# The S5 input projection channel-major, with its recurrence rows gathered through DRAM

## The chip, the cores and the metric

The kernel runs on one core of one Trainium2 chip. The metric is the time of one execution on the device in microseconds (us), as the median of several runs. A lower time is better. The engines are named as in the profile: PE is the matrix engine, PEld its weight loads, DVE the vector engine, ACT the scalar engine, POOL GpSimd. SP is SyncE, which issues every DMA of this kernel in one queue.

## The reference

The trunk has two layers on 512 tokens of 1024 channels, in float32. Each layer has three mixers beside each other and an MLP:

```python
for l in range(DEPTH):                                   # 2 layers
    z = _rmsnorm(x, norm_mix_g[l]) @ w_in[l]             # 1024 -> 2508 columns
    q, k, v, qi, ki, wi, u5, z_ssd, xbc, dt_raw = _split(z, IN_SIZES)
    attn_out = _dsa_mixer(q, k, v, qi, ki, wi, ...)      # 8 heads; an indexer keeps the top 128 keys
    s5_out = _s5_mixer(u5, ...)                          # 256 channels = 16 groups of 16
    ssd_out = _ssd_mixer(z_ssd, xbc, dt_raw, ...)
    x = x + concat(attn_out, s5_out, ssd_out) @ w_out[l]
    x = x + relu(_rmsnorm(x) @ w_up[l]) ** 2 @ w_down[l]
```

The S5 mixer runs, in every group of 16 channels, a diagonal complex recurrence of 64 states over the 512 tokens, reads it out, adds `d_skip * u`, and passes the result through gelu and a gated linear unit (GLU).

## The kernel before

**Order of the work.** The kernel is written as generators, one for each strand (the projection slab by slab, the S5 strand, the SSD strand, attention, the top-k of the indexer). A planner at build time advances whichever strand its own costs, priorities and due times choose, and so fixes the order of the instructions on every engine. On the chip each engine then works through its list in that order, and an instruction whose input is late holds up all behind it. The plan of the slices is `kv, xa, qi, q, xb, u5, z` in layer 0 and `kv, xa, qi, z, u5, q, xb` in layer 1.

**Products.** Weights come in slabs of 256 KB (`wraw`, line 159). ACT writes the high part (`whi`, line 171), DVE the low part (`wlo`, line 172); three raw and five split slabs are held. Each product of 128 rows is three matmuls (`mm3`, lines 436 to 438). `gemm_tok` gives token-major tiles, with 128 tokens as the stationary operand and the columns of the slab moving. `gemm_chan` gives channel-major tiles of 128 channels by 512 tokens, with 128 columns of the slab stationary and 512 tokens moving. Four PSUM banks (`pm`) hold the tiles of the projection.

**The S5 input before.** The slice `u5` (256 columns) is token-major, in four tiles whose tokens lie four apart. They leave PSUM at line 1186 (`usb`, on ACT), scaled per token by `rsp`, for which the strand sums squares once more (`tsum`, line 397) and takes a reciprocal root on DVE (`rsqrt`, lines 299 to 305).

**The S5 strand** (`s5`, line 671) works on chunks of 8 tokens. It wants `U`, two tiles for 8 groups each, whose row is (token within the chunk, channel within the group) and whose columns are groups by 64 chunks. Before, PE transposes `usb` (line 684) and ACT copies the halves out (lines 687 and 688). Then come the chunk sums on PE (`s5v`, line 699), ACT's evictions (`sv`, `svs`), a rotation and eight scans for each half on DVE (lines 714 to 726, which end in the two `X` tiles), PE's read-out (`s5y`, lines 738 and 739), the transposes back, gelu and the GLU (lines 750 to 775).

**Around it.** The table matrices `M` are zeroed by POOL (line 663) and filled by eight DMAs each from `strip` (line 666). The last `M` of layer 1 takes over a slot that `s5v` reads. The indexer's scores are `isc`; a round of its top-k is one MAX and one MATCH_REPLACE on DVE (lines 1076 and 1077), 16 rounds for each of the blocks 1, 2 and 3 of 128 tokens, and line 1080 makes the mask that attention waits for.

Of the kernel before, what the change touches and what calls it, by code (L numbers as in the profile page):

```python
# [10 lines left out]
F32 = mybir.dt.float32  # L11
# [11 lines left out]
NB = S // P          # token blocks  # L23
KC = D // P          # channel chunks of the trunk
# [83 lines left out]
# constants  # L108
# [8 lines left out]
# W_in slices: (first column, width), in the host's column order  # L117
# [17 lines left out]
class Slabs:  # L135
    """slabs of weight matrices in the order of their use: loaded and split into hi and lo parts some way ahead"""
# [44 lines left out]
    def take(self, n, tiles, outer):  # L181
        """the next n slabs for each of some tiles, as (tile, slab number, hi, lo): slab by slab if outer, else
        tile by tile, and then those to follow are split while the last tile uses these up"""
        if outer:
            for j in range(n):
                hi, lo = self.next()[0]
                for t in range(tiles):
                    yield t, j, hi, lo
            return
        cur = []  # L190
        for t in range(tiles):
            for j in range(n):
                if t == 0:
                    cur += self.next()
                elif t == tiles - 1:
                    self.load(self.i + AHEAD[0] + j)
                    self.split(self.i + AHEAD[1] + j)
                yield t, j, cur[j][0], cur[j][1]


class Net:
    def __init__(self, ctx, tc, a, taps=None):
# [91 lines left out]
    def rsqrt(self, y, x, n, eng=None):  # L294
        """y = 1/sqrt(x), [P, n] small"""
# [11 lines left out]
    def stt(self, v, out, x, s, y, op0, op1):  # L307
        """out = (x op0 s) op1 y, [P, n] small; GpSimd takes two instructions for it"""
# [7 lines left out]
    def expacc(self, out, x, t, v):  # L316
        """out = exp(x) to about an ulp, [P, n] small"""
# [15 lines left out]
    def sincos(self, c, s, th, t, v):  # L333
        """c, s = cos(th), sin(th), [P, n] small"""
# [14 lines left out]
        self.stt(v, q, q, 1.0, r, ALU.add, ALU.mult)      # sin(th/2)  # L349
# [4 lines left out]
        # cos(th/2) = 1 + w  # L354
# [9 lines left out]
    def norm_chunk(self, c, squares=True):  # L364
        """hi and lo parts of x*g, and the sum of squares over channels (still per partition)"""
# [25 lines left out]
    def token_sums(self, acc, perm=False):  # L391
        """[P, 4]: mean square + eps per token; block b is tokens b*128 + m, or with perm 4m + 3-b"""
        nc = self.nc
        p = self.ps("a", (P, 4), name="tsum")
        v = acc.rearrange("p (m f) -> p f m", f=4)
        for b in range(NB):
            nc.tensor.matmul(p[:, b:b + 1], v[:, 3 - b, :] if perm else acc[:, b * P:(b + 1) * P], self.ones[:, 0:1],
                             start=True, stop=True)
# [4 lines left out]
    def bcast_tokens(self, colv, k):  # L403
        """[P, 4] per-token columns -> psum tile [P, 512] with the token's value on every partition"""
# [6 lines left out]
    def add_slabs(self, l):  # L411
        """the weights of a layer, in the order of their use"""
# [20 lines left out]
    def mm3(self, p, lh, ll, rh, rl, first, last):  # L433
        """p += (lh+ll)^T (rh+rl), without the product of the two low parts (below float32's last bit)"""
# [5 lines left out]
    def gemm_tok(self, ps, xh, xl, slabs, sls):  # L440
        """token-major blocks: psum tile of block i [tok, n] = ps(i), tokens sls[i]; yields (cost, finished tile)"""
# [14 lines left out]
    def gemm_chan(self, ps, slabs, xh, xl):  # L456
        """channel-major tiles of 128 columns of a slice of 256: [chan, tok]; yields (cost, finished tile)"""
# [13 lines left out]
    def s5_small(self):  # L471
        """powers of the discretised state matrix and the input matrices, both layers"""
# [38 lines left out]
        # powers 0..8  # L511
# [17 lines left out]
        # X = (pr; pi), Y = (-pi; pr) on the two halves of the partitions  # L529
# [8 lines left out]
        # m8 and the rotation of one chunk, with the angle's sign turned on the lower half  # L538
# [4 lines left out]
        self.rot = []          # e^{+-i phi 2^k}  # L543
# [22 lines left out]
    def s5_tables(self, l, t):  # L566
        """the matrices of one layer's chunked recurrence, into t"""
# [29 lines left out]
        def outer(v, out, u, w, u2, w2, gs, d0, d1):  # L597
            """out[g, d, h] = u[g, h] w[g, d] + u2[g, h] w2[g, d]"""
# [9 lines left out]
        for q in range(4):  # L608
# [4 lines left out]
            BPp = self.tt([P, 4, 8, 16], name="BPp")               # d = 1..8: the states stand one step ahead  # L613
            outer(v, BPp, bbr, X, bbi, Y, gs, 1, 9)
            # transposed input powers: rows (d, h')
# [8 lines left out]
        # rotations by chunk  # L624
# [21 lines left out]
        for q in range(4):  # L646
            v = eng(f"C{q}")
            gs = slice(4 * q, 4 * q + 4)
            ca = self.tt([P, 4, 8, 16], name="CA")                 # d = 0..7
# [7 lines left out]
            # the skip term joins the kernel's first tap  # L657
# [14 lines left out]
    def s5(self, l, tab, usb, out):  # L672
        """usb: token-major input -> hi/lo of the two channel-major output tiles"""
# [5 lines left out]
        # input with rows (d = 7-i, h')  # L679
        U = [self.h([P, 8, C5], name="U5") for _ in range(2)]  # L680
        for q4 in range(4):
            p = self.ps(self.bank["sU"], (64, 4, P), name="s5U")
            for j in range(4):
                nc.tensor.transpose(p[:, j], usb[q4 // 2][:, (4 * q4 + j) % 8].rearrange("p b h -> p (b h)"), self.ident)
            pv = p.rearrange("p g (c e) -> p g c e", e=2)
            o = slice(4 * (q4 % 2), 4 * (q4 % 2) + 4)
            nc.scalar.activation(U[q4 // 2][0:64, o], pv[:, :, :, 1], AF.Copy)
            nc.scalar.activation(U[q4 // 2][64:128, o], pv[:, :, :, 0], AF.Copy)
            yield self.pace["s5"] * 1.0
# [38 lines left out]
        # rows (half of the groups, chunk)  # L728
# [16 lines left out]
        # channel-major, columns (token of the chunk, half, chunk)  # L745
        gg = []
        for jh in range(2):
# [8 lines left out]
            v.scalar_tensor_tensor(t, t, 1.0, p, ALU.add, ALU.mult)      # 2 gelu(y)  # L756
# [25 lines left out]
    def ssd(self, l, r_, out):  # L782
# [3 lines left out]
        # step sizes  # L786
# [37 lines left out]
        # convolution and silu, each with half the argument  # L824
        xc = {}
        for m in (0, 1, 2, 3) if self.plan["w_order"].index("xa") < self.plan["w_order"].index("xb") else (2, 3, 0, 1):
# [16 lines left out]
            else:  # L843
                # C of each group, with zeros on the other group's partitions
# [21 lines left out]
            # token-major inputs  # L866
# [12 lines left out]
            # scores  # L879
# [33 lines left out]
        # gate and group norm  # L913
# [55 lines left out]
    def head_ms(self, out, src, nh):  # L969
        """mean square over the 64 of each head, + eps"""  # L970
# [6 lines left out]
    def rope(self, x, rs, c, s):  # L977
        """x = rope(x * rs * gain), of the keys"""
# [8 lines left out]
    def rope_q(self, x, c, s):  # L987
        """the rotated part of eight heads' queries"""
# [8 lines left out]
    def attn_keys(self, l, ksb, rt):  # L997
        """ksb: [P, 3, 64] per block (k0 k1 ki): norm, rope, transposes"""
# [7 lines left out]
        # hi and lo parts of the keys, each on both halves of the partitions  # L1006
# [18 lines left out]
    def transpose_heads(self, src):  # L1025
        """[P, 8, 64] token-major -> per head [P (hi d, lo d), P tokens]"""
# [15 lines left out]
    def head_dot(self, p, q, K, i, nk):  # L1042
        """p[tok, key] = q . k, both with all of their bits"""
# [3 lines left out]
    def index_scores(self, b, qi, K, wi, accs):  # L1047
        """masked scores of block b (>= 1): [P, (b+1)*128]"""
# [21 lines left out]
    def topk_masks(self, accs):  # L1070
        """the 128 largest of each row (lowest index first among equals) keep 0, the rest get NEG"""
# [10 lines left out]
    def attend(self, b, qT, K, mask, nrs, ah, al):  # L1082
        """nrs: minus the scale of each head's logits"""
# [450 lines left out]
```

## Time and profile before

| | us |
|---|---|
| median of 3 runs (1359.14 to 1361.53) | 1359.96 |
| span of the profiled execution | 1356.7 |
| difference, taken as fixed time around the span | 3.3 |
| layer 0: mixers, MLP | 0 to 355, 355 to 715 |
| layer 1: mixers, MLP | 715 to 985, 985 to 1357 |
| PE busy over the span | 1247.9 (92%) |
| DVE busy over the span | 883.2 (65%) |
| mean granted clock of PE, as a share of full speed | 0.967 |

The profile shows one execution. Busy times are sums over the span, and a share that is high over the whole can be low in one stage. The record of one matmul is longer than the distance between the starts of two, since matmuls overlap; so a row of matmuls is priced by the starts.

### The profile page before, as it was taken

How to read it: one execution, taken by the hardware profiler on the slowest of the kernel's cores; microseconds unless marked ns; L12 is line 12 of the kernel's file. 1: busy time of each engine (PE TensorE's matmuls, PEld its weight loads, DVE VectorE, ACT ScalarE, POOL GpSimd, SP SyncE). 2: the span in 40 equal slices, each digit the busy share in tenths (PEclk: the TensorE clock that was granted, in tenths of full speed). 3: DMA queues.
4: the chain of work that ended last, by engine and by line, in shares of the span. 5: the costliest groups of instructions: out<-in, count | busy, mean ns of one | idle time of the engine just before them, and what ended most of it. 6: DMA issues, size and time to landing. Idle time of an engine off the chain costs nothing. (4 is left out here: it accounts for less than half of the span.)

```text
span 1356.7 us, 17071 instructions
## 1 busy us (share of the span) xinstructions
PE 1247.9 (92%) x5852; PEld 1013.6 (75%) x5852; DVE 883.2 (65%) x2044; ACT 564.6 (42%) x1160; POOL 161.6 (12%) x301
## 2 busy tenths in 40 slices
PE   6679966879999999999999998978999999999998
PEld 5667854647888877888888897755688888888887
DVE  6899799884844544444466779998575444445443
ACT  4346352563542332423444535656454233242331
POOL 2593268200000221000000000000000000000000
PEclk9789987899999999999999998989999999999999
DMA  6122120001233323323323312100123333333332
GB/s 193 47 78 71 25 68 11 32 1 47 86 95 100 94 83 94 101 96 99 94 84 89 100 31 53 63 16 16 35 83 102 95 99 94 101 94 101 93 108 86
DMA packets 102694, 103.74 MB, mean 76 GB/s; under 512 B 10960, under 2 KB 95696, under 8 KB 102608
## 3 DMA queue, kind: packets, MB, share of 16 engines
q1 hardware_dynamic: 102608, 102.66, 25.1%
q8 instruction: 46, 0.75, 0.2%
q14 instruction: 40, 0.33, 0.1%
HBM read 99.36 MB, written 2.10 MB: 75 GB/s over the span
## 5 line engine op out<-in xcount | busy, mean ns | idle before, releaser
L172 DVE TENSOR_TENSOR wlo<-wraw,whi 128x512 fp32r<-128x512 f32 (+1 forms) x368 | 253.8, 691 | 300.6 <-ACT whi L171 298.4
L171 ACT ACTIVATE whi<-wraw 128x512 fp32r<-128x512 f32 (+1 forms) x368 | 229.0, 624 | 498.5 <-PE pm L437 332.4
L436 PE MATMUL pm<-xh,whi 128*128 128x512 f32 x608 | 239.8, 395 | 2.7 <-ACT usb L1186 1.1
L437 PE MATMUL pm<-xl,whi 128*128 128x512 f32 x608 | 238.5, 393 | 0.0
L438 PE MATMUL pm<-xh,wlo 128*128 128x512 f32 x608 | 238.4, 393 | 0.0
L438 PE MATMUL pm<-uh,wlo 128*128 128x512 f32 x512 | 199.5, 390 | 1.2 <-DVE wlo L172 1.2
L437 PE MATMUL pm<-ul,whi 128*128 128x512 f32 x512 | 199.7, 390 | 0.0
L436 PE MATMUL pm<-uh,whi 128*128 128x512 f32 x512 | 199.6, 390 | 0.0
L436 PEld LDWEIGHTS pm<-xh,whi 128*128 128x128 f32 x608 | 115.2, 190 | 27.6 <-ACT q L1210 1.6
L438 PEld LDWEIGHTS pm<-xh,wlo 128*128 128x128 f32 x608 | 115.1, 189 | 24.4 <-issue 0.3
L437 PEld LDWEIGHTS pm<-xl,whi 128*128 128x128 f32 x608 | 115.3, 190 | 23.1 <-DVE xl L372 0.2
L438 PEld LDWEIGHTS pm<-uh,wlo 128*128 128x128 f32 x512 | 96.2, 188 | 21.7 <-DVE wlo L172 1.6
L436 PE MATMUL pm<-whi,xh 128*128 128x512 f32 (+2 forms) x240 | 94.1, 395 | 19.8 <-ACT xh L370 12.4
L437 PEld LDWEIGHTS pm<-ul,whi 128*128 128x128 f32 x512 | 96.2, 188 | 20.3 <-issue 0.4
L436 PEld LDWEIGHTS pm<-uh,whi 128*128 128x128 f32 x512 | 96.2, 188 | 19.9 <-issue 0.2
L437 PE MATMUL pm<-wlo,xh 128*128 128x512 f32 (+2 forms) x240 | 92.5, 386 | 2.3 <-DVE wlo L172 2.3
L438 PE MATMUL pm<-whi,xl 128*128 128x512 f32 (+2 forms) x240 | 92.2, 388 | 1.5 <-DVE xl L372 1.4
L436 PEld LDWEIGHTS pm<-whi,xh 128*128 128x128 f32 x240 | 55.9, 234 | 27.1 <-ACT xh L370 12.8
L437 PEld LDWEIGHTS pm<-wlo,xh 128*128 128x128 f32 x240 | 56.3, 235 | 7.6 <-DVE wlo L172 3.4
L438 PEld LDWEIGHTS pm<-whi,xl 128*128 128x128 f32 x240 | 55.7, 234 | 7.1 <-DVE xl L372 2.5
L1384 DVE SCALAR_TENSOR_TENSOR ur<-pm,ur 128x512 f32<-128x512 f32 x64 | 44.0, 687 | 25.5 <-ACT ur L1381 25.5
L1392 DVE TENSOR_TENSOR sq<-pm,r2b 128x512 f32<-128x512 f32 x64 | 44.2, 690 | 23.2 <-PE pm L438 23.2
(349 smaller groups left out, 1915.2 us busy)
## 6 DMA issues: line engine op xcount, KB each, us to landing
wraw<-in_w_up_dram SPq DMA_DIRECT2D x128, 256.0 KB, 2.7
wraw<-in_w_down_dram SPq DMA_DIRECT2D x128, 256.0 KB, 2.7
wraw<-in_w_in_dram SPq DMA_DIRECT2D x64, 256.0 KB, 2.7
wraw<-in_w_out_dram SPq DMA_DIRECT2D x32, 256.0 KB, 2.7
wraw<-in_w_in_dram SPq DMA_DIRECT2D x16, 166.0 KB, 2.3
x<-in_xT_dram SPq DMA_DIRECT2D x8, 256.0 KB, 5.9
out_dram<-x SPq DMA_DIRECT2D x8, 256.0 KB, 2.0
s5bc<-in_s5bc_dram SPq DMA_DIRECT2D x4, 256.0 KB, 4.7
```

What stands on the lines that cost most here:

```text
L171: nc.scalar.activation(hi, raw, AF.Copy)
L172: nc.vector.tensor_tensor(lo, raw, hi.bitcast(F32), ALU.subtract)
L436: nc.tensor.matmul(p, lh, rh, start=first, stop=False)
L437: nc.tensor.matmul(p, lh, rl, start=False, stop=False)
L438: nc.tensor.matmul(p, ll, rh, start=False, stop=last)
L1384: v.scalar_tensor_tensor(r, p, 0.0, r, ALU.max, ALU.mult)
L1392: v.tensor_tensor(t, d[1], rb, ALU.mult)
```

## The change

The slice `u5` goes through `gemm_chan` instead of `gemm_tok`. Its two tiles are multiplied by `rb` (the row of reciprocal roots that `z` and the SSD inputs use as well) in the eviction on DVE, with the tokens put in the order (token within the chunk, chunk). Each tile is written to a DRAM buffer, and eight DMAs read it back as `U`, 16 rows each. The own token sums, the reciprocal root, the transposes and their copies go.

```diff
-    def s5(self, l, tab, usb, out):
+    def s5(self, l, tab, U, out):
...
-        U = [self.h([P, 8, C5], name="U5") for _ in range(2)]
-        for q4 in range(4):
-            p = self.ps(self.bank["sU"], (64, 4, P), name="s5U")
-            for j in range(4):
-                nc.tensor.transpose(p[:, j], usb[q4 // 2][:, (4 * q4 + j) % 8].rearrange("p b h -> p (b h)"), self.ident)
...
-            nc.scalar.activation(U[q4 // 2][0:64, o], pv[:, :, :, 1], AF.Copy)
-            nc.scalar.activation(U[q4 // 2][64:128, o], pv[:, :, :, 0], AF.Copy)
...
-                    msp = self.token_sums(self.nrm[2], True)
-                    r["rsp"] = self.s([P, 4], tag="rsp", bufs=1)
-                    self.rsqrt(r["rsp"], msp, 4)
...
-                    nc.scalar.activation(r["usb"][hf][:, :, i], p[:, hf * P:(hf + 1) * P].rearrange("p (g h) -> p g h", h=16),
-                                         AF.Copy, scale=r["rsp"][:, i:i + 1])
...
+                if k[0] == "u":
+                    v.tensor_tensor(t.rearrange("p (d c) -> p d c", d=T5), p.rearrange("p (c d) -> p d c", d=T5),
+                                    r["rb"].rearrange("p (c d) -> p d c", d=T5), ALU.mult)
+                    dr = self.dp.tile([P, T5, C5], F32, tag="u5", name=self.nm("u5d"), bufs=2)
+                    nc.sync.dma_start(dr, t.rearrange("p (d c) -> p d c", d=T5))
+                    u = self.h([P, 8, C5], name="U5")
+                    for d in range(T5):
+                        nc.sync.dma_start(u[16 * d:16 * d + 16], dr.rearrange("(g h) d c -> d h g c", h=16)[T5 - 1 - d])
+                    r.setdefault("U", []).append(u)
```

The planner's costs are not touched, but its strands now come ready at other moments, and the order shifts on several engines. Three places in layer 1 follow.

PE, at the end of `u5`. Before, a first product of `q` (`pm` from `whi`, `xh`), then the transposes `s5U`, then the chunk sums of both halves (`s5v`) and two `M` products:

```order
L438 MATMUL pm_1853_7747<-whi_1840_7679,xl_1528_6379 128x512
L684 MATMUL s5U_1857_7755<-cons_85,usb_1847_7710 64x128 x4
L684 MATMUL s5U_1858_7762<-cons_85,usb_1847_7710 64x128 x4
L684 MATMUL s5U_1859_7769<-cons_85,usb_1848_7711 64x128 x4
L684 MATMUL s5U_1860_7776<-cons_85,usb_1848_7711 64x128 x4
L699 MATMUL s5v_1865_7787<-U5_1855_7753,BPT_1114_4614 128x128 x4
L699 MATMUL s5v_1866_7795<-U5_1855_7753,BPT_1120_4637 128x128 x4
L699 MATMUL s5v_1867_7806<-U5_1856_7754,BPT_1132_4673 128x128 x4
L699 MATMUL s5v_1868_7814<-U5_1856_7754,BPT_1141_4703 128x128 x4
L738 MATMUL s5y_1877_7867<-M5_1214_4920,U5_1855_7753 64x128
L738 MATMUL s5y_1878_7886<-M5_1225_4967,U5_1855_7753 64x128
```

Now (line numbers are smaller by 1 or 12), after 15 matmuls of `q`, the chunk sums of half 0, two `M` products, the chunk sums of half 1, then `q` again:

```order
L437 MATMUL pm_1841_7609<-whi_1887_7846,xl_1562_6482 128x512
L687 MATMUL s5v_1847_7619<-U5_1833_7572,BPT_1105_4531 128x128 x4
L687 MATMUL s5v_1848_7627<-U5_1833_7572,BPT_1111_4554 128x128 x4
L726 MATMUL s5y_1859_7699<-M5_1205_4837,U5_1833_7572 64x128
L726 MATMUL s5y_1860_7718<-M5_1216_4884,U5_1833_7572 64x128
L687 MATMUL s5v_1849_7638<-U5_1836_7591,BPT_1123_4590 128x128 x4
L687 MATMUL s5v_1850_7646<-U5_1836_7591,BPT_1132_4620 128x128 x4
L435 MATMUL pm_1874_7787<-whi_1829_7558,xh_1518_6294 128x512
```

Both halves of `U` are now awaited from DMAs, and the second one behind the first. After the last row 22 more matmuls of `q` stand ahead of the read-out that needs the first `X`.

DVE, where the S5 recurrence stands. Before, a top-k row, then rotation and scans of both halves, with the top-k of blocks 2 and 3 largely still to come:

```order
L1076 MAX mx1_1920_8093<-isc_1734_7266 128x8
L714 TENSOR_TENSOR sv_1861_7783<-sv_1861_7783,COS_1146_4718 128x512
L711 MEMSET X5_1869_7825 128x8
L715 TENSOR_TENSOR svs_1863_7785<-svs_1863_7785,SIN_1147_4719 128x512
L1077 MATCH_REPLACE isc_1734_7266<-mx1_1920_8093,isc_1734_7266 128x256
L716 TENSOR_TENSOR sv_1861_7783<-sv_1861_7783,svs_1863_7785 128x512
L714 TENSOR_TENSOR sv_1862_7784<-sv_1862_7784,COS_1176_4807 128x512
L720 SCALAR_TENSOR_TENSOR sw_1871_7831<-s5m8_185,sv_1861_7783 128x64 x8
L715 TENSOR_TENSOR svs_1864_7786<-svs_1864_7786,SIN_1177_4808 128x512
L711 MEMSET X5_1870_7826 128x8
```

Now, the last top-k rows of block 3 (`mx3`, `isc` of 512 columns), then the first scan and the way to the first `X`:

```order
L1064 MAX mx3_2166_8837<-isc_1775_7343 128x8
L1065 MATCH_REPLACE isc_1775_7343<-mx3_2166_8837,isc_1775_7343 128x512
L699 MEMSET X5_1851_7657 128x8
L708 SCALAR_TENSOR_TENSOR sw_1853_7663<-s5m8_187,sv_1843_7615 128x64 x8
L1068 TENSOR_SCALAR isc_1775_7343<-isc_1775_7343 128x512
L699 MEMSET X5_1852_7658 128x8
L702 TENSOR_TENSOR sv_1844_7616<-sv_1844_7616,COS_1167_4724 128x512
L703 TENSOR_TENSOR svs_1846_7618<-svs_1846_7618,SIN_1168_4725 128x512
L712 TENSOR_TENSOR sw_1853_7663<-sw_1853_7663,COS_1137_4635 128x512
L713 TENSOR_TENSOR sws_1854_7672<-sws_1854_7672,SIN_1138_4636 128x512
L704 TENSOR_TENSOR sv_1844_7616<-sv_1844_7616,svs_1846_7618 128x512
L714 TENSOR_TENSOR X5_1851_7657<-sw_1853_7663,sws_1854_7672 128x8x63
```

Between the eviction of the second `u5` tile and the scan stand 69 top-k rows (5 MAX and 5 MATCH_REPLACE of 256 columns, 13 and 14 of 384, 16 and 16 of 512), three masks and the three rotation rows of half 0. No top-k row of the layer comes after it.

SP, the DMA queue. Before, the last slabs of `q`, the GLU weights, then the eight pieces of the last `M`:

```order
L159 DMA wraw_1909_8036<-in_w_in_dram 128x512
L678 DMA glw_1854_7751<-in_s5_glu_w_dram 128x2x256
L666 DMA M5_1241_5036<-strip_1239_5031 16x512
L666 DMA M5_1241_5036<-strip_1239_5031 16x4x112
L666 DMA M5_1241_5036<-strip_1239_5031 16x4x96
L666 DMA M5_1241_5036<-strip_1239_5031 16x4x80
L666 DMA M5_1241_5036<-strip_1239_5031 16x4x64
L666 DMA M5_1241_5036<-strip_1239_5031 16x4x48
L666 DMA M5_1241_5036<-strip_1239_5031 16x4x32
L666 DMA M5_1241_5036<-strip_1239_5031 16x4x16
```

Now the write of the first tile, its eight gathers (one row, x8), the write of the second, one gather of it, then the GLU weights and `M`:

```order
L159 DMA wraw_1890_7865<-in_w_in_dram 128x512
L1178 DMA u5d_1832_7570<-u5_1831_7568 128x512
L1181 DMA U5_1833_7572<-u5d_1832_7570 16x8x64 x8
L1178 DMA u5d_1835_7589<-u5_1834_7587 128x512
L1181 DMA U5_1836_7591<-u5d_1835_7589 16x8x64
L677 DMA glw_1842_7613<-in_s5_glu_w_dram 128x2x256
L665 DMA M5_1232_4953<-strip_1230_4948 16x512
L665 DMA M5_1232_4953<-strip_1230_4948 16x4x112
L665 DMA M5_1232_4953<-strip_1230_4948 16x4x96
L665 DMA M5_1232_4953<-strip_1230_4948 16x4x80
L665 DMA M5_1232_4953<-strip_1230_4948 16x4x64
L665 DMA M5_1232_4953<-strip_1230_4948 16x4x48
L665 DMA M5_1232_4953<-strip_1230_4948 16x4x32
L665 DMA M5_1232_4953<-strip_1230_4948 16x4x16
L1181 DMA U5_1836_7591<-u5d_1835_7589 16x8x64 x7
```

The other seven gathers of the second tile have come to stand behind the eight pieces of `M`, whose memset on POOL waits for a chunk sum of half 0.

In layer 0 the order moves in the same manner: the pieces of two `M` tiles, which wait for POOL, stand between the writes and gathers, and 18 more top-k rows come ahead of the first rotation.

## Rows read from the trace of the kernel before

**Rows 1.** The page: span, and busy time of each engine.

```profile
span 1356.7 us, 17071 instructions
...
PE 1247.9 (92%) x5852; PEld 1013.6 (75%) x5852; DVE 883.2 (65%) x2044; ACT 564.6 (42%) x1160; POOL 161.6 (12%) x301
```

**Rows 2.** Windows, the two mixer stages (columns: window, PE, PEld, DVE, ACT, POOL, clock).

```profile
0.00:355.00 355.00, 283.24 (x1381) 224.27 (x1382) 296.69 (x840) 167.66 (x388) 139.59 (x266) 0.91 0.20 57
...
715.00:985.00 270.00, 240.74 (x1239) 191.43 (x1239) 214.09 (x639) 140.99 (x341) 0.52 (x1) 0.95 0.18 51
```

**Rows 3.** Windows inside the two mixer stages, same columns.

```profile
190.00:230.00 40.00, 19.22 (x107) 15.41 (x105) 38.41 (x75) 10.39 (x20) 37.34 (x72) 0.82 0.09 26
860.00:985.00 125.00, 104.36 (x527) 74.52 (x526) 99.26 (x297) 68.09 (x177) 0.00 (x0) 0.93 0.10 32
```

**Rows 4.** Timeline of PE, layer 1 (start, us, instruction, idle before).

```profile
782.80 0.39 PE L437 MATMUL pm<-xl,whi 128*128 128x512 f32 x1
783.03 0.40 PE L438 MATMUL pm<-xh,wlo 128*128 128x512 f32 x1
783.26 0.28 PE L436 MATMUL pm<-whi,xh 128*128 128x256 f32 x1
...
811.46 0.40 PE L437 MATMUL pm<-wlo,xh 128*128 128x256 f32 x1
811.70 0.40 PE L438 MATMUL pm<-whi,xl 128*128 128x256 f32 x1
817.32 0.80 PE L436 MATMUL pm<-whi,xh 128*128 128x512 f32 x1 [5.23 <-ACT usb L1186]
...
818.77 3.62 PE L684 MATMUL s5U<-cons,usb 128*64 128x128 f32 x16
822.18 4.07 PE L699 MATMUL s5v<-U,BPT 128*128 128x128 f32 x32
...
858.58 0.39 PE L438 MATMUL pm<-whi,xl 128*128 128x512 f32 x1
```

**Rows 5.** Timeline of PE's weight loads, layer 1.

```profile
782.35 0.19 PEld L436 LDWEIGHTS pm<-xh,whi 128*128 128x128 f32 x1
...
806.20 0.33 PEld L438 LDWEIGHTS pm<-whi,xl 128*128 128x128 f32 x1
```

**Rows 6.** Timeline of DVE, layer 1.

```profile
797.38 0.68 DVE L1199 SCALAR_TENSOR_TENSOR z<-pm,rb 128x512 f32<-128x512 f32 x1
...
834.37 0.68 DVE L726 TENSOR_TENSOR X<-sw,sws 128x504 f32<-128x504 f32 x1
...
839.68 0.68 DVE L726 TENSOR_TENSOR X<-sw,sws 128x504 f32<-128x504 f32 x1
```

**Rows 7.** DVE groups by form between 860 and 985 us.

```profile
L1076 DVE MAX8 mx<-isc 128x8 f32<-128x512 f32 x12 | 8.2, 684 | 0.0
L1077 DVE MATCH_REPLACE8 isc<-mx,isc 128x512 f32<-128x512 f32 x12 | 8.1, 674 | 0.0
...
L1076 DVE MAX8 mx<-isc 128x8 f32<-128x384 f32 x3 | 1.6, 545 | 0.0
L1077 DVE MATCH_REPLACE8 isc<-mx,isc 128x384 f32<-128x384 f32 x3 | 1.6, 537 | 0.0
```

**Rows 8.** Timeline of SyncE's queue (SPq), both layers.

```profile
158.93 13.84 SPq L666 DMA_DIRECT2D M<-strip  x12
...
824.18 5.55 SPq L666 DMA_DIRECT2D M<-strip  x8
```

**Rows 9.** DMA issues: size, us from issue to landing.

```profile
out_dram<-x SPq DMA_DIRECT2D x8, 256.0 KB, 2.0
...
M<-strip SPq DMA_DIRECT2D x8, 32.0 KB, 1.9
```

**Rows 10.** Timeline of POOL, layer 1.

```profile
823.63 0.52 POOL L663 MEMSET M<- 128x512 f32 x1 [299.88 <-PE s5v L699]
```

**Rows 11.** Timeline of DVE, layer 0.

```profile
162.09 0.16 DVE L400 TENSOR_SCALAR ms<-tsum 128x4 f32<-128x4 f32 x1 [3.37 <-PE tsum L397]
```

More of the change, by code (lines that the diff above doesn't have):

```diff
@@ L212, in __init__ @@
         self.sp = e(tc.tile_pool(name="sp", bufs=4))
+        self.dp = e(tc.tile_pool(name="dp", bufs=2, space=bass.MemoryType.DRAM))
         self.pp = {k: e(tc.tile_pool(name=f"p{k}", bufs=n, space=PSUM)) for k, n in BANKS.items()}
@@ L389, in norm_end, with token_sums @@
         return self.nrm[:3]
-    def token_sums(self, acc, perm=False):
+    def token_sums(self, acc):
         nc = self.nc
         p = self.ps("a", (P, 4), name="tsum")
-        v = acc.rearrange("p (m f) -> p f m", f=4)
         for b in range(NB):
-            nc.tensor.matmul(p[:, b:b + 1], v[:, 3 - b, :] if perm else acc[:, b * P:(b + 1) * P], self.ones[:, 0:1],
-                             start=True, stop=True)
+            nc.tensor.matmul(p[:, b:b + 1], acc[:, b * P:(b + 1) * P], self.ones[:, 0:1], start=True, stop=True)
         ms = self.s([P, 4], tag="ms", bufs=2)
@@ L678, in s5 @@
         nc.sync.dma_start(glw, self.a["s5_glu_w"][l].rearrange("(k p) n -> p k n", p=P))
-        U = [self.h([P, 8, C5], name="U5") for _ in range(2)]
-        for q4 in range(4):
-            p = self.ps(self.bank["sU"], (64, 4, P), name="s5U")
-            for j in range(4):
-                nc.tensor.transpose(p[:, j], usb[q4 // 2][:, (4 * q4 + j) % 8].rearrange("p b h -> p (b h)"), self.ident)
-            pv = p.rearrange("p g (c e) -> p g c e", e=2)
-            o = slice(4 * (q4 % 2), 4 * (q4 % 2) + 4)
-            nc.scalar.activation(U[q4 // 2][0:64, o], pv[:, :, :, 1], AF.Copy)
-            nc.scalar.activation(U[q4 // 2][64:128, o], pv[:, :, :, 0], AF.Copy)
-            yield self.pace["s5"] * 1.0
         hb = [self.h([P, 8, C5], name="sv") for _ in range(2)]
@@ L1176, in done @@
         def done(k, i, p):
-            if k == "u5":
-                if "usb" not in r:
-                    msp = self.token_sums(self.nrm[2], True)
-                    r["rsp"] = self.s([P, 4], tag="rsp", bufs=1)
-                    self.rsqrt(r["rsp"], msp, 4)
-                    r["usb"] = [self.h([P, 8, NB, 16], name="usb") for _ in range(2)]
-                for hf in range(2):
-                    nc.scalar.activation(r["usb"][hf][:, :, i], p[:, hf * P:(hf + 1) * P].rearrange("p (g h) -> p g h", h=16),
-                                         AF.Copy, scale=r["rsp"][:, i:i + 1])
-            elif k[0] in "xz":
+            if k[0] in "xzu":
                 if "rb" not in r:
@@ L1194, in done @@
                 t = self.g(name=k)
-                if k[0] == "x":
+                if k[0] == "u":
[7 more added lines that the diff above has]
+                    r.setdefault("U", []).append(u)
+                elif k[0] == "x":
                     v.tensor_tensor(t, p, r["rb"], ALU.mult)
@@ L1253, in trunk_in @@
             pm = lambda: self.ps(bank, name="pm")[:, :n]
-            if k[0] in "xz":
+            if k[0] in "xzu":
                 gemm = self.gemm_chan(lambda: self.ps(bank, name="pm"), slabs, xh, xl)
-            elif k == "u5":
-                gemm = self.gemm_tok(pm, xh, xl, slabs, [slice(3 - b, S, 4) for b in range(NB)])
             else:
@@ L1317, in recurrent @@
             yield self.start["s5"]
-            yield from self.s5(l, self.tab, r["usb"], out)
+            yield from self.s5(l, self.tab, r["U"], out)
         else:
```

## The prediction

> **What bounds the kernel now.** I read the page first. PE is busy for 92% of the span [rows 1], and the reader is to see that this is a mean over stages. The windows by stage come next: PE is busy for 283.2 of 355 us in the mixers of layer 0 and for 240.7 of 270 us in those of layer 1 [rows 2]. The MLPs do not contain the change, so its gain or loss falls in these two stages. The smaller windows tell who holds PE up. Between 190 and 230 us, behind the S5 input of layer 0, PE is busy for 19.2 and DVE for 38.4 of 40 us; between 860 and 985 us PE for 104.4 and DVE for 99.3 of 125 us [rows 3]. Behind the point of the change DVE is thus nearly full in both layers, and PE often waits. The timeline of PE in layer 1 shows the place itself: `u5` from 783.3 to 811.9, an idle 5.23 us in which PE waits for `usb`, the transposes from 818.8, the chunk sums from 822.2, and the last matmul of `q` at 858.6 [rows 4]. The timeline of DVE gives the two `X` tiles at 834.4 and 839.7, ready 0.7 us later [rows 6].
>
> **The projection itself.** Before, 96 matmuls of 256 columns start 0.24 us apart (811.46 and 811.70). A channel-major matmul of 512 columns, as `z` has just ahead, takes 0.23 us (782.80, 783.03, 783.26) [rows 4]. The weight load explains it: 0.33 us each for the stationary tokens that lie four apart, 0.19 us for a slab's columns [rows 5]. So 96 x 0.235 = 22.6 us become 48 x 0.23 = 11.0 us, 11.5 us less PE work per layer. The Trainium skill ("TensorE: Matmul & The Clock Gate", section "Back-to-back issue gap") prices the isolated gap by the columns, 256 at half of 512; by that rule PE would save nothing here. The rows above contradict it for these matmuls, and I keep it as a rival only.
>
> **What else goes.** The 16 transposes of a layer take 3.4 us (818.77 to 822.18) [rows 4]; ACT's evictions and copies stand beside other work. On DVE twelve rows of about 0.16 us for the reciprocal root go, and in layer 0 the 3.37 us that it waits for the token sums [rows 11]. Two evictions come, about 0.65 us each by that of `z` [rows 6]. Their reordering read of PSUM is not in the trace; it lies between the 0.65 us and twice that, 1.3 us, and I take 0.65 us, since the wider `X` rows with strides cost 0.68 us as well [rows 6].
>
> **The DRAM round trip.** No such transfer is in the trace. For the write I take the store of an output tile of the same 256 KB, landed 2.0 us after issue; for a gather the 32 KB piece of `M`, landed after 1.9 us [rows 9]. SP spends 5.55 us on eight such pieces, 0.69 us each [rows 8]. One half of `U` so takes 0.6 + 2.0 + 5.6 + 1.9 = 10 us, from below 4.5 us (if issues cost nothing beyond the two landings) and from above 14 us (if both landings are twice as long). I take 10, since issue times repeat across rows. The Trainium skill ("DMA: Bandwidth & Descriptors", section "Specifications") wants pieces of at least 512 bytes for line rate, and the gathers' pieces have 256; whether a gather from DRAM suffers, no run here shows, and by that rule the upper end would be the price.
>
> **Layer 1 in order of time.** (1) `u5` ends 11.5 us earlier, at about 800.5, and the 15 matmuls of `q` in hand end at 804. (2) Some 12 rows of 0.6 us stand on DVE between the `z` eviction at 797.4 and the first eviction of `u5`, and seven to the second: these end at about 806 and 811. (3) Half 0 of `U` lands at 816, and its chunk sums, half of 4.07 us [rows 4], end at 818. (4) Only now may POOL clear the last `M` (0.52 us, released by `s5v` [rows 10]); its eight pieces take SP until 824, the seven gathers behind them 4.9 us more, and half 1 lands at 831. PE idles 12 us and 13 us, where it idled 5.2 us. Up to here the 11.5 + 3.4 us that PE saved are spent: `q` goes on at 833, where the chunk sums before ended at 826.3.
>
> (5) What is late next is DVE. Behind the second eviction stand the 69 top-k rows of the remaining rounds. By its records a round of 512 columns costs 1.36 us and one of 384 costs 1.08 us [rows 7]; one of 256 I put at 0.8 us by proportion. So 16 x 1.36 + 13.5 x 1.08 + 5 x 0.8 = 40.3 us is an upper bound, since records of neighbours overlap; I take 37.6 us, and 2.9 us for three masks and three rotations. The scan starts at 811 + 40.5 = 851.5, the first `X` is ready at about 857, the second at 862.5; before, 835.1 and 840.4. PE has 23 matmuls of `q` in hand at 833, ends them at 839, and waits 18 us. Queued behind that read-out is all the rest of `q`, and attention waits for the whole of `q`. (6) Before, `q` ended (858.6 + 0.23) 18.4 us behind the second `X`. Now 40 matmuls of it are left there where 46 were, 1.4 us less: it ends at about 880, 21 us later.
>
> (7) What gives time back. From 859 to 985 PE had 104.4 us of work and 20.6 us of idle, and DVE spent 8.2 + 8.1 + 1.6 + 1.6 = 19.5 us, with the loads of the values some 20.6 us, on top-k rounds [rows 3, 7], which are all done by 851 now. If PE never waited, the mixers would end at 880 + 104 = 984, or some 4 us earlier at the full clock, since the mean was 0.93 there [rows 3]: 980. If it waited as before, at 1006. I take 6 us of waiting at the old clock, 990, near the lower end, because DVE's load in this stretch falls from 79% to 63%. Layer 1 ends **5 us later**, between -5 and +21.
>
> **Layer 0.** DVE sets the pace here, so the 11.5 us of PE are covered by DVE's work [rows 3] and count only if that cover is gone. DVE saves the wait of 3.4 us and 1.9 us of small rows and pays 1.3 us: **4 us earlier**. From one side the bound is all of PE's 11.5 us. From the other: SP's twelve pieces of `M`, some of which wait for POOL, lasted until 172.8 (158.93 + 13.84) [rows 8], and the second gathers now stand behind pieces of that series. Half 1 of `U` lands near 179. The top-k rows that have moved ahead of the rotation hide that; if they do not and DVE waits for `U` as long as it did for the token sums, the saving is gone and 3 us are lost: between -11.5 and +3.
>
> **Sum.** 1356.7 - 4 + 5 = 1357.7 us for the span, and with the 3.3 us by which the median of the runs stands over the profiled span, 1361.0 us.
>
> **Rivals.** *Faster: the late S5 is covered.* PE idled 20.6 us behind `q`, mostly in the shadow of a full DVE that now has 20.6 us less to do. If the tail runs dense at 980 and layer 0 gives 8 us, the time is 1356.7 - 5 - 8 + 3.3 = 1347 us. Against it: the last chain of attention passes from engine to engine, and lighter DVE does not shorten it. It decides when less than 1 us of waiting remains in the tail, or when the second `X` comes before about 850. *Slower: nothing is given back.* The stall in which PE waits for the first `X` behind DVE's top-k (step 5) goes through in full: 1356.7 - 4 + 15 to 21 + 3.3 gives 1371 to 1377 us. For it speaks that the order of attention behind `q` is the same, against it the 20.6 us. It decides when over 14 us of waiting remain in the tail. The landing of the gathers is no part of it: half 1 may land 20 us later than 831 before the scan at 851.5 would notice. *The change does not do what it says.* If the matmuls of 512 columns cost twice those of 256, as the page's rule has it, `u5` ends at 812 still, steps (2) to (6) come 9 to 10 us later, and the time is near 1370 us; the starts in [rows 4] speak against it.
>
> **How the numbers follow.** A measurement of this kernel tells about 0.2%, 2.7 us, from no change. The forecast (a loss in layer 1 about as large as the gain in layer 0) has 0.45, with a range of its own of 1354 to 1368 us: of that 0.07 faster, 0.20 the same, 0.18 slower. The faster rival has 0.30 (0.02 of it within 0.2%), the slower one 0.22, the last 0.03. Faster 0.35, same 0.22, slower 0.43. The range of 1346 to 1375 us takes in the faster rival and half of the slower one.
>
> **What would show it.** Right: matmuls of `u5` with 512 columns 0.23 us apart; PE idle for about 12 us twice around 804 to 831, then near 839 to 857 with `X` as what it waits for; DVE full of top-k until 851; `q` ended near 880; the last mask near 852; the mixers ended near 990. In layer 0 the end of the mixers near 351. Wrong: scans that come before 845, gathers that land in over 10 us, a layer 0 that moves by more than 8 us, or a tail behind `q` shorter than 100 or longer than 120 us.

## The result, and the profile after

The changed kernel takes 1366.97 us (median of 4 runs, 1364.94 to 1368.85), the kernel before 1359.55 us beside it (4 runs, 1357.59 to 1361.53): **slower**, ratio 1.0053, 95% interval 1.0035 to 1.007. The profiled span grows by 6.5 us:

```profile
span 1363.2 us, 16779 instructions
...
PE 1220.0 (89%) x5708; PEld 978.7 (72%) x5708; DVE 880.9 (65%) x2024; ACT 553.5 (41%) x1128; POOL 157.8 (12%) x301
```

PE has 27.9 us less to do than in [rows 1] and the kernel is still slower. The two layers go opposite ways. In the table the end of a mixer stage is the start of DVE's last eviction into `x`, and layer 1 starts with its first projection matmul:

| us | before | after |
|---|---|---|
| layer 0: mixers end | 356.06 | 345.59 |
| layer 1 starts | 713.78 | 703.23 |
| layer 1, from its start: first and second `X` ready | 121.3, 126.6 | 142.9, 149.2 |
| layer 1, from its start: last matmul of `q` | 144.8 | 167.0 |
| from there to the end of the mixers | 154.2 | 149.2 |

Layer 0 gains 10.5 us, layer 1 loses 22.2 us up to the end of `q` and gets 5.0 back behind it: -10.5 + 17.2 = 6.7 us, the 6.5 of the span.

The windows after, the first two as in [rows 2] (columns: window, PE, PEld, DVE, ACT, POOL, clock):

```profile
0.00:355.00 355.00, 278.05 (x1363) 214.21 (x1364) 298.94 (x844) 166.79 (x381) 135.72 (x266) 0.91 0.22 63
715.00:985.00 270.00, 211.26 (x1069) 160.23 (x1068) 206.98 (x613) 129.30 (x315) 0.52 (x1) 0.89 0.17 48
800.00:850.00 50.00, 18.54 (x70) 15.27 (x71) 46.97 (x129) 9.23 (x24) 0.52 (x1) 0.59 0.09 23
```

The last row shows where the loss lies: for 50 us behind the S5 input PE works 18.5 us and DVE 47.0. The timeline of PE there, with what ended each idle time in brackets (it answers to [rows 4]):

```profile
788.05 0.39 PE L436 MATMUL pm<-xl,whi 128*128 128x512 f32 x1
788.27 0.39 PE L437 MATMUL pm<-xh,wlo 128*128 128x512 f32 x1
...
801.16 3.78 PE L687 MATMUL s5v<-U,BPT 128*128 128x128 f32 x16 [9.10 <-DMA U<-u5d]
...
814.32 3.75 PE L687 MATMUL s5v<-U,BPT 128*128 128x128 f32 x16 [8.33 <-DVE mx L1064]
...
842.89 0.80 PE L435 MATMUL pm<-whi,xh 128*128 128x512 f32 x1 [21.97 <-ACT svs L693]
```

The first two rows are the last of `u5`; 15 matmuls of `q` follow. Then come three idle times, 9.1, 8.3 and 22.0 us, where [rows 4] had one of 5.2. In the second, `mx` is only the last event of a wait for several; SyncE's queue names the late one:

```profile
793.85 0.33 SPq L1178 DMA_DIRECT2D u5d<-u  x1
795.91 3.74 SPq L1181 DMA_DIRECT2D U<-u5d  x8
799.75 0.38 SPq L1178 DMA_DIRECT2D u5d<-u  x1
801.88 0.30 SPq L1181 DMA_DIRECT2D U<-u5d  x1
802.23 0.43 SPq L677 DMA_DIRECT2D glw<-in_s_glu_w_dram  x1
803.85 5.07 SPq L665 DMA_DIRECT2D M<-strip  x8
808.96 3.42 SPq L1181 DMA_DIRECT2D U<-u5d  x7
```

Seven gathers of half 1 leave only at 809, behind the pieces of `M`, as the order had it. DVE gives the third idle time (compare [rows 6]):

```profile
839.03 0.28 DVE L708 TENSOR_TENSOR_SCAN sw<-s5m,sv 128x64 f32<-128x64 f32 x1
839.22 1.36 DVE L708 TENSOR_TENSOR_SCAN sw<-s5m,sv 128x64 f32<-128x64 f32 x7
...
845.41 0.68 DVE L714 TENSOR_TENSOR X<-sw,sws 128x504 f32<-128x504 f32 x1
```

And ACT, between DVE and PE:

```profile
840.61 0.63 ACT L710 ACTIVATE sws<-sw 64x512 f32<-64x512 f32 x1 [23.05 <-DVE sw L708]
841.15 0.31 ACT L691 ACTIVATE sv<-s5v 128x192 f32<-128x192 f32 x1
...
842.62 0.22 ACT L693 ACTIVATE svs<-s5v 64x64 f32<-64x64 f32 x1
```

The scan stands behind the last top-k rows of block 3; ACT's copy `sws` waits 23 us for it; the last evictions of half 1's chunk sums stand behind that copy on ACT, and `q` on PE behind them.

### The profile page after: what moved, and what is told of

Same layout as the page of the kernel before. It is cut to its first block, busy times and chain, and to the rows that moved or that the text cites. A ratio compares the mean times of both kernels' runs of the same rounds, so it can differ in the third digit from the quotient of the medians.

```text
span 1363.2 us, 16779 instructions
## 1 busy us (share of the span) xinstructions
PE 1220.0 (89%) x5708; PEld 978.7 (72%) x5708; DVE 880.9 (65%) x2024; ACT 553.5 (41%) x1128; POOL 157.8 (12%) x301
## 5 line engine op out<-in xcount | busy, mean ns | idle before, releaser
L435 PE MATMUL pm<-xh,whi 128*128 128x512 f32 x640 | 252.5, 395 | 1.5 <-ACT q L1198 1.5
L436 PE MATMUL pm<-xl,whi 128*128 128x512 f32 x640 | 251.1, 393 | 0.0
L437 PE MATMUL pm<-xh,wlo 128*128 128x512 f32 x640 | 250.7, 392 | 0.0
L437 PE MATMUL pm<-uh,wlo 128*128 128x512 f32 x512 | 199.3, 390 | 1.2 <-DVE wlo L172 1.2
L435 PEld LDWEIGHTS pm<-xh,whi 128*128 128x128 f32 x640 | 121.3, 190 | 28.9 <-ACT q L1198 2.2
L436 PEld LDWEIGHTS pm<-xl,whi 128*128 128x128 f32 x640 | 121.2, 189 | 24.4 <-issue 0.2
L435 PEld LDWEIGHTS pm<-uh,whi 128*128 128x128 f32 x512 | 96.1, 188 | 20.1 <-issue 0.2
L435 PE MATMUL pm<-whi,xh 128*128 128x512 f32 (+1 forms) x176 | 68.8, 394 | 34.6 <-ACT svs L693 22.0
L436 PE MATMUL pm<-wlo,xh 128*128 128x512 f32 (+1 forms) x176 | 67.8, 386 | 3.1 <-DVE wlo L172 3.1
L437 PE MATMUL pm<-whi,xl 128*128 128x512 f32 (+1 forms) x176 | 67.7, 390 | 2.3 <-DVE xl L373 2.3
L435 PEld LDWEIGHTS pm<-whi,xh 128*128 128x128 f32 x176 | 35.6, 203 | 41.1 <-ACT svs L693 22.4
L1370 DVE SCALAR_TENSOR_TENSOR ur<-pm,ur 128x512 f32<-128x512 f32 x64 | 44.0, 687 | 25.5 <-ACT ur L1367 25.5
L1372 DVE TENSOR_TENSOR ul<-ur,uh 128x512 fp32r<-128x512 f32 x64 | 44.0, 688 | 22.4 <-ACT uh L1371 22.4
L435 PE MATMUL pm<-mh,whi 128*128 128x512 f32 x128 | 51.2, 401 | 1.4 <-DVE x L1340 1.4
```

Of the source, the lines that this page charges most:

```text
L435: nc.tensor.matmul(p, lh, rh, start=first, stop=False)
L436: nc.tensor.matmul(p, lh, rl, start=False, stop=False)
L437: nc.tensor.matmul(p, ll, rh, start=False, stop=last)
L1370: v.scalar_tensor_tensor(r, p, 0.0, r, ALU.max, ALU.mult)
L1372: v.tensor_tensor(lo, r, h.bitcast(F32), ALU.subtract)
```

## The experiments

All compare with runs of the kernel before on the same chip (1358.2 to 1358.6 us). The edits are made to the changed kernel with a switch per layer, `NEW`, that selects the old or the new S5 input.

**Each layer alone.**

```diff
-NEW = (True, True)
+NEW = (True, False)    # e1_layer0_only; (False, True) in e2_layer1_only
```

> The change in layer 0 alone; layer 1 takes its S5 input as before. Theory A (the two layers add, the loss is made in layer 1 alone): the mixers of layer 0 end 10 to 11 us earlier, layer 1 is as before, so the time is 1359.6 - 10.5 = 1349 us. Rival B (layer 0's gain is bought with something that layer 1 pays back, slots or queue entries that come free later): 1355 us or more.

> The change in layer 1 alone. Theory A: layer 0 as before, layer 1 longer by 17 us: 1376 to 1377 us, with PE idle about 20 us for the rotated chunk sums, and the first X ready some 22 us later than before. Rival B: the late start of layer 1 is part of it, and the loss without layer 0's change is under 10 us: below 1370 us.

Measured: layer 0 alone 1351.35 us, ratio 0.9953 (0.9937 to 0.9969); layer 1 alone 1374.78 us, 1.0126 (1.0098 to 1.0155). The layers nearly add up: -6.8 and +16.6 us against +7.4 for both. The gain of layer 0 and the loss of layer 1 are shown apart. Layer 0 alone fell a little short of theory A: its mixers end 8.3 us earlier, at 347.8.

**Layer 1: the order on DVE.** In `e3` the top-k of block 3 in layer 1 waits for the second `X` by a tiny DVE row; in `e5` the top-k of blocks 2 and 3 waits from round 4 of block 2 on, counted from 0 (`e5` is the base of `e6` to `e8`). The edit of `e3`:

```diff
+            if bl == (3,) and self.plan is PLAN[1]:
+                while "X" not in r:
+                    yield None
+                a3 = r["acc"][3]
+                self.nc.vector.scalar_tensor_tensor(a3[:, 0:1], r["X"][:, 0, 1:2], 0.0, a3[:, 0:1], ALU.mult, ALU.add)
```

> The changed kernel, but in layer 1 the top-k of block 3 waits for the second X tile (a small DVE instruction that adds 0 times a value of X to one column of the scores). The round trip through DRAM stays. Theory A1 (layer 1 loses by the order on DVE, where the scans stand behind all the top-k): the second X is ready near 832 instead of 852, the product q ends near 852 instead of 870, the time is near 1352 us. Rival B1 (layer 1 loses by the round trip itself, the waits for U): the waits of 9 and 8 us for U stay and q ends no more than 5 us earlier; 1362 us or more.

> As e3, but in layer 1 the top-k of blocks 2 and 3 waits for the second X from round 4 of block 2 on. It is the control for the next three, which have the same order on DVE. The scans now stand right behind the 13 rows that finish block 1, so X is bound by the arrival of U alone. If the order on DVE was all of the loss (A1), the time is that of e3 or less, 1350 to 1356 us, with the same two waits for U of about 9 and 8 us.

Measured: 1355.22 us (`e3`, 0.9979, 0.9967 to 0.9991) and 1351.52 us (`e5`, 0.9955, 0.9937 to 0.9972). PE's waits for `U` stay at 17.6 us in `e3`, but the third one shrinks:

```profile
801.40 3.78 PE L701 MATMUL s5v<-U,BPT 128*128 128x128 f32 x16 [9.26 <-DMA U<-u5d]
814.49 3.75 PE L701 MATMUL s5v<-U,BPT 128*128 128x128 f32 x16 [8.29 <-DMA U<-u5d]
823.31 0.80 PE L437 MATMUL pm<-whi,xh 128*128 128x512 f32 x1 [2.73 <-ACT svs L707]
```

Little but the order moved, and 22.0 us of waiting became 2.7. As theory A1 had it, the second `X` is ready at 832.5 and `q` ends at 850.1 (the profiled execution took 1351.59 us, 3.6 less than the median). From the start of the layer the last `q` comes at 146.9 us, where it was 144.8 before and 167.0 after: the order on DVE made 20.1 of the 22.2 us lost up to the end of `q`. The tail behind `q` is 156.0 us instead of 149.2, so of the 17.2 us that the layer lost as a whole 13.4 come back.

**Layer 1: the round trip.** `e4` fills `U` by an ACT copy from the tile, without the DRAM buffer and the permutation of the rows. `e6` issues every second gather of layer 1 from ACT's queue. `e7` gives the pool of S5's table matrices (`t`), from which `M` and the `BPT` that the chunk sums read take their slots, a seventeenth slot, and takes one from the general pool (`g`); `e8` has both.

```diff
-                    dr = self.dp.tile([P, T5, C5], F32, tag="u5", name=self.nm("u5d"), bufs=2)
...
+                    nc.scalar.activation(u, t.rearrange("p (d c) -> p d c", d=T5), AF.Copy)     # e4
...
-                        nc.sync.dma_start(u[16 * d:16 * d + 16], ...)
+                        (nc.scalar if l and d % 2 else nc.sync).dma_start(u[16 * d:16 * d + 16], ...)     # e6
...
-GBUFS = {"g": 52, "t": 16}
+GBUFS = {"g": 51, "t": 17}     # e7
```

> The changed kernel without the write, the DRAM buffer and the gathers: U is filled by two copies on ACT straight from the evicted tiles, so the rows of U are not permuted (the permutation is left out). Theory A1: the order on DVE also moves, since U is there early, and layer 1 gains all: 1335 to 1345 us. Rival B1 gives about the same time; the two differ in what e3 shows. A third view (the tail behind q sets the end whatever comes before): not below 1350 us.

> e5 with every second gather of layer 1 issued by ACT instead of SP. If the round trip is bound by issuing (0.5 us each in one queue), half 0 lands 2 us earlier and half 1 some 4 us earlier, and the time falls by 2 to 4 us against e5; if it is bound by landing, or ACT's own work is held up by it, no change or slower.

> e5 with a slot of its own for the last M of layer 1, so that its eight pieces are issued in layer 0's time and no longer stand between the gathers of half 1. If they are what makes half 1 late, its sums start about 6.5 us earlier (8.3 us of waiting become 2) and the time falls by 3 to 6 us against e5. If the waits before the scans are covered by what follows, no change.

> e6 and e7 together. If both waits count, 1345 to 1350 us, towards the 1341 us of the kernel without the round trip; if the end of the mixers is set by the tail behind q, no better than the better one of e6 and e7.

| | us | ratio (95%) | waits before the chunk sums | last `q` from layer start | tail |
|---|---|---|---|---|---|
| e4 | 1341.22 | 0.9879 (0.9856 to 0.9901) | 2.5, for ACT's copy | 124.8 | 165.5 |
| e5 | 1351.52 | 0.9955 (0.9937 to 0.9972) | 17.3 | 142.3 | 160.0 |
| e6 | 1346.64 | 0.9913 (0.9898 to 0.9929) | 13.9 | 138.6 | 159.2 |
| e7 | **1339.26** | 0.9857 (0.9841 to 0.9872) | 11.4 | 135.3 | 159.1 |
| e8 | 1342.05 | 0.9873 (0.9855 to 0.9891) | 9.8 | 133.6 | 160.0 |

The slot cuts the second wait from 8.3 to 2.4 us. With sixteen slots the last `M` waits for the slot of a `BPT` that half 0's chunk sums still read; with seventeen POOL clears it in layer 0's time (at 505.6) and the gathers of half 1 no longer stand behind its pieces. SyncE in `e7`:

```profile
798.93 0.30 SPq L1212 DMA_DIRECT2D U<-u5d  x1
...
799.77 3.30 SPq L1212 DMA_DIRECT2D U<-u5d  x7
```

The two queues shorten the waits by 3.4 us in `e6`. On top of the slot the intervals of `e7` and `e8` overlap: nothing more is shown. Of the 12.3 us between `e5` and `e7`, 7.8 lie in layer 1; most of the rest lies in layer 0, where `e7` (342.73) and `e8` (345.35), the same there, differ by nearly as much, so it is not assigned. Three expectations were off: `e6` gained 4.9 us on `e5` (2 to 4 expected), `e7` 12.3 (3 to 6), and `e8` came out below its 1345 to 1350 us, though no better than `e7`.

**The slot without the gate, and without the change.** `e11` is the changed kernel with the slot alone; `e12` the kernel before with it.

```diff
-GBUFS = {"g": 52, "t": 16}
+GBUFS = {"g": 51, "t": 17}     # e11: NEW = (True, True); e12: NEW = (False, False)
```

> The changed kernel with a seventeenth slot for M and the halves of U, and no gate: the S5 rows still stand behind the top-k of block 3 on VectorE. Theory A: VectorE's order is the larger part of the loss of layer 1 and the slot helps only in layer 0 and a little in layer 1: 1355 to 1363, the scan still after 845 - 10 = 835 us. Rival B: the late second half of U is the cause and the order follows it: 1339 to 1346, as with the gate and the slot.

> The kernel before with a seventeenth slot in the pool of M (there no half of U uses the pool). Theory A: the slot is worth something only because the change put the halves of U in front of M in that pool: 1357 to 1361, as before. Rival B: the wait of M for its slot already cost time before the change, and the 12 us gained by the slot are no matter of the change: 1346 to 1353.

Measured: `e11` 1356.69 us (0.9972, 0.9955 to 0.9989), `e12` 1361.03 us (1.0009, 0.9996 to 1.0022). The two expectations speak of halves of `U` in `M`'s pool. By the code that is not so: the halves lie in the general pool before and after the change, and what `M` and they share is SyncE's queue. Before the change no gather stands behind `M`'s pieces in that queue, and the slot is worth nothing. With the change it is worth 9 to 11 us (by the medians and by the ratios). Not all of this is the slot's own: in `e11` only 60 top-k rows stand ahead of the scan, not 69, and it started at 830.8, earlier than theory A had it. The pair `e5` and `e7`, with one order of DVE around the scan, is the cleaner one. The wait behind DVE stays in `e11`, now seen at the read-out itself:

```profile
836.69 0.48 PE L741 MATMUL s5y<-CA,X 128*64 128x128 f32 x1 [21.22 <-DVE X L728]
```

The gate takes that away as well: `e7` beats both kernels.

**Layer 0: whose time was it?** `e9` is the kernel before, `e10` is `e1`, each with one edit in layer 0.

```diff
-                    msp = self.token_sums(self.nrm[2], True)
...
+                        r["rsp"] = rstd()     # e9
...
+                if twice:     # e10, u5 only
+                    self.mm3(p, wh[:, i, c], wl[:, i, c], xh[k], xl[k], k == 0, False)
```

> The kernel before, in layer 0 without the S5 input's own token sums, root and small rows: usb is scaled with the rstd that the other inputs use, so each token with another token's scale (this part of the computation is left out). Theory A: half of layer 0's 10.5 us comes from DVE, which waited 3.4 us for these token sums and no longer has to: layer 0's last x eviction near 351 us (before 356.1), the time near 1354. Rival B: the gain of layer 0 is TensorE's saved half of the projection: nothing moves here, last x eviction 355 to 357, time 1358 to 1360.

> Layer 0 alone changed, and its S5 projection's matmuls issued twice (the sum halved in the eviction), so that TensorE's saved 11.5 us of layer 0 are taken back and all else stays changed. Theory A: the saved matmuls are the gain of layer 0: last x eviction back from 347.8 to 356 to 359 us, time 1358 to 1362. Rival B: the gain is the order and the transposes: the time stays at 1351 to 1354. Between the two (1355 to 1357): both have a share.

| layer 0, us | before | e9 | e10 | e1 | after | e7 |
|---|---|---|---|---|---|---|
| first `X` ready | 194.5 | 188.8 | 196.4 | 193.0 | 192.1 | 189.6 |
| second `X` ready | 206.7 | 200.6 | 210.3 | 199.3 | 198.4 | 195.9 |
| first rotation starts | 181.4 | 176.2 | 182.2 | 180.7 | 179.8 | 180.4 |
| from there to the second `X` | 25.3 | 24.4 | 28.1 | 18.6 | 18.6 | 15.5 |
| POOL busy in that stretch | 21.1 | 17.2 | 25.5 | 7.6 | 7.6 | 0.0 |
| mixers end | 356.1 | 351.1 | 357.4 | 347.8 | 345.6 | 342.7 |

`e9` took 1355.75 us (0.9976, 0.9963 to 0.9988), `e10` 1362.02 us (1.0024, 1.0011 to 1.0037). Without the own token sums the mixers end 4.9 us earlier. `e10` ends where its theory A put it, but it does not set PE apart. With the matmuls issued twice the first rotation starts only 1.5 us later than in `e1`; the way from there to the second `X` is 9.5 us longer, and there the same rows of DVE take 9.4 us more (the scan of half 0 4.35 us, that of half 1 2.78). The order around them moved as well, and POOL is busy beside them, for 9.77 us of the ten from 190 on, where `e1` has 0.07. POOL in `e10`:

```profile
190.00:200.00 10.00, 9.77 (x11) 0.83 0.09 28
```

So it is not shown that PE's saved matmuls are the gain. What runs through all six is the second `X`, 147 to 151 us ahead of the end, and the way to it, which is longer the longer POOL is busy in it. (The second `X` alone does not settle the end: in `e4` it is ready at 189.2 and the mixers end at 347.2, 158 us later.) DVE shows why the second `X` comes so much earlier than the first. Before:

```profile
189.45 2.65 DVE L716 TENSOR_TENSOR sv<-sv,svs 128x512 f32<-128x512 f32 x1
192.02 2.46 DVE L726 TENSOR_TENSOR X<-sw,sws 128x504 f32<-128x504 f32 x1
194.41 5.66 DVE L720 TENSOR_TENSOR_SCAN sw<-s5m,sv 128x64 f32<-128x64 f32 x8
...
201.47 1.52 DVE L724 TENSOR_TENSOR sw<-sw,COS 128x512 f32<-128x512 f32 x1
...
203.00 1.45 DVE L725 TENSOR_TENSOR sws<-sws,SIN 128x512 f32<-128x512 f32 x1
```

After, with the same rows (the earlier scan is that of half 0):

```profile
181.35 1.43 DVE L704 TENSOR_TENSOR sv<-sv,svs 128x512 f32<-128x512 f32 x1
182.81 3.73 DVE L708 TENSOR_TENSOR_SCAN sw<-s5m,sv 128x64 f32<-128x64 f32 x8
...
191.38 0.68 DVE L714 TENSOR_TENSOR X<-sw,sws 128x504 f32<-128x504 f32 x1
191.97 1.56 DVE L708 TENSOR_TENSOR_SCAN sw<-s5m,sv 128x64 f32<-128x64 f32 x8
...
195.18 0.69 DVE L712 TENSOR_TENSOR sw<-sw,COS 128x512 f32<-128x512 f32 x1
```

The rows are the same size. The windows of POOL beside them, before:

```profile
190.00:200.00 10.00, 9.84 (x18) 0.83 0.12 23
```

After:

```profile
190.00:200.00 10.00, 1.15 (x1) 0.84 0.25 80
```

POOL builds the tables of layer 1 there. Before, their input `s5bc` was issued at 177.70. After, SyncE issues the pieces of `U` and `M` until 180.94, 5.0 us later than those of `M` before, and three slabs of `w_out` ahead of `s5bc` take 14.1 us more:

```profile
180.99 14.13 SPq L159 DMA_DIRECT2D wraw<-in_w_out_dram  x3
195.17 0.46 SPq L560 DMA_DIRECT2D s5bc<-in_s5bc_dram  x1
```

So POOL rests while half 1 is scanned. The five rows shown of before are 9.4 us longer than such rows beside an idle POOL (2.0, 1.8, 4.1, 0.8, 0.8), and the scan of half 0 there, 1.98 us, is 0.4 longer. After, the stretched rows are those of half 0: 0.75 and 2.2 us too long, with 0.2 for two more, 3.1 in all. So DVE spends 9.4 + 0.4 - 3.1 = 6.7 us less, and the first rotation starts 1.6 us earlier: the 8.3 us of the second `X`. In `e9` POOL is busy for 9.53 of those 10 us and the scan of half 1 takes 5.65; in `e7` POOL does nothing between the first rotation and the second `X`, and the scans take 1.57 and 1.56. No run moved POOL alone, so this cause is read from the durations of six runs and not tested by itself.

## Why the prediction was right, and where it was off

The time lies in the range (1361.0 forecast, 1367.0 measured), on the side that had the largest chance, and the place of the loss was the one named. Two terms were mis-sized, in opposite ways: layer 1 lost 17.2 us where 5 were forecast, layer 0 gained 10.5 where 4 were. That the sum is off by 6 us only is in part luck, since half of the first error is covered by the second. Two of the prediction's own signs of being wrong came: layer 0 moved by more than 8 us, and the tail behind `q` is longer than 120 us.

- **The projection.** Right: the last matmuls of `u5` start 0.22 to 0.23 us apart, those of 256 columns before started 0.24 us apart. The Trainium skill ("TensorE: Matmul & The Clock Gate", section "Back-to-back issue gap"), whose isolated gap would make them twice those of 256 columns, is not borne out here.
- **The round trip, steps (3) and (4).** From the issue of the write to the first chunk sum it took 7.3 us (793.85 to 801.16), 10 forecast, within 4.5 to 14. The landings were as taken (2.1 us for the write, 1.9 for a gather, below), and the doubled landings of the upper end did not come; the term that was too large is SyncE's issue, 0.47 us for a gather where the sum had 0.69. The idle times were 9.1 and 8.3 us for 12 and 13. The eviction took 1.04 us in layer 1, inside its bounds.
- **DVE's order, step (5).** Right. In the time of before (10.55 us later) the scan started at 849.6, the `X` tiles were ready at 856.6 and 863.0; forecast 851.5, 857, 862.5. PE waited 22 us for 18, at another hop: for ACT's evictions behind the scan's copy, not for `X` at the read-out, and with 8 matmuls of `q` in hand instead of 23.
- **`q`, step (6).** 22.2 us later, 21 forecast.
- **What gives time back, step (7): the step that failed.** Forecast 16 us, measured 5.0; the sum took 6 us of waiting, and 16.8 remained. (The 985 that was taken for the end of the mixers before is 28 us early: the last eviction into `x` starts at 1012.8. PE is never idle between the two, so the 20.6 us of idle time stand, but the tail of 100 to 120 us was too short by as much.) The reason given was that DVE's load behind `q` falls. It did: 123.4 us of work in the 155 before, 105.4 in the 150 after. But PE's idle time only fell from 20.6 to 16.8 us, by the windows of before and after:

```profile
858.00:1013.00 155.00, 134.36 (x665) 99.15 (x664) 123.35 (x335) 84.81 (x206) 0.00 (x0) 0.94 0.14 42
```

```profile
870.00:1020.00 150.00, 133.21 (x665) 97.14 (x663) 105.40 (x286) 85.04 (x206) 0.00 (x0) 0.95 0.14 43
```

The waits there are not for a full DVE. After `q`, before:

```profile
PE ssds L883 <- DVE CT L848: 6.0, 1, 6.0
PE pTp L1113 <- ACT pe L1105: 5.4, 5, 2.4
PE ssdT L870 <- DVE cv L841: 3.0, 1, 3.0
PE ssdy L897 <- DVE dec L886: 2.7, 1, 2.7
```

After (columns: us in total, times, longest):

```profile
PE ssds L871 <- DVE CT L836: 5.7, 1, 5.7
PE pTp L1101 <- ACT pe L1093: 3.0, 3, 2.4
PE ssdy L885 <- DVE dec L874: 2.7, 1, 2.7
```

Two of the largest are one step of a chain each and stayed; what went is the wait for DVE's `cv` (3.0) and some of the waits for ACT's `pe` (2.4). So for layer 1 the rival "nothing is given back" was right: its sign, over 14 us of waiting left in the tail, came, and 17.2 lies in its 15 to 21 us. Its time was missed only because it kept the -4 us of layer 0. The reason, that a lighter DVE does not shorten such a chain, stood in the prediction against the faster rival. In the other direction the tail gives little too: with `q` 20 us earlier (`e4`) it grows by 11.3 us.

- **Layer 0.** Forecast -4, bounds -11.5 to +3, measured -10.5. The term that was named, DVE's wait and small rows, is worth 4.9 alone (`e9`); in the changed kernel the first rotation starts only 1.6 us earlier, with 18 more top-k rows ahead of it. The term that the prediction did not have is POOL: some 6.7 us by which its rest shortens DVE's rows on the way to the second `X`. The last 2.2 of the 10.5 us lie behind the second `X` and stay open. That DVE covers PE's saving is neither shown nor refuted: in `e10` PE's work is back and the first rotation moves by 1.5 us, but POOL's work came back beside DVE with it.

## What to carry to other kernels

Before crediting a saved stretch on one engine, list what the scheduler now puts ahead of the next link on the slowest engine: here 69 top-k rows ahead of the scan cost PE 22.0 us of waiting, the DMA round trip 17.4. Price a give-back by the waits that remain and who releases each, not by an engine's load. When transfers that wait for a buffer stand in one queue ahead of transfers that an engine waits for, count the slots of that buffer: one more slot and a gate on the order turned a loss of 0.5% into a gain of 1.4%.

## What the runs showed of the hardware

A gather of 32 KB in 256-byte pieces lands as fast as a piece of `M` of the same size. Issues after:

```profile
u5d<-u SPq DMA_DIRECT2D x4, 256.0 KB, 2.1
U<-u5d SPq DMA_DIRECT2D x32, 32.0 KB, 1.9
...
M<-strip SPq DMA_DIRECT2D x8, 32.0 KB, 1.9
```

DVE rows with two tensor inputs took 2 to 4 times as long in stretches in which POOL was busy: 2.46 us instead of 0.68 for `X`, 5.66 instead of 1.56 for eight scans. The Trainium skill ("SBUF — State Buffer", section "SBUF: two separate sides") says that DVE operations with two inputs in SBUF and GpSimd's reads take turns on a port pair, one blocked while the other holds it. The durations agree.

The long idle time cost once more behind its end. The matmuls of `q` behind the 22 us start 0.43 us apart at first, with a granted clock of 0.52 (the level of 1.2 GHz) from 842.0 to 847.6, and 0.23 us apart after that, with 1.00 (2.4 GHz) up to 870:

```profile
844.76 0.63 PE L435 MATMUL pm<-whi,xh 128*128 128x512 f32 x1
845.19 0.63 PE L436 MATMUL pm<-wlo,xh 128*128 128x512 f32 x1
...
847.60 0.39 PE L436 MATMUL pm<-wlo,xh 128*128 128x512 f32 x1
847.83 0.39 PE L437 MATMUL pm<-whi,xl 128*128 128x512 f32 x1
```

That is ten matmuls with 0.2 us more each, about 2 us that the stall in step (5) brought with it and no term of the sum held.
